# Joined quarters in the entry, transposed modulation columns, routing without GpSimd, and a split last bank

## The chip, the cores and the metric

The program runs on one core of a Trainium2 chip. The metric is the device time of one execution in microseconds (us). The engines are TensorE (PE in the profile), VectorE (DVE), ScalarE (ACT), GpSimd (POOL) and SyncE (SP), whose queue issues the loads.

## The reference

Two blocks run one after the other on 256 tokens of width 1024, all in float32. The first has two layers; each modulates a normalised input, mixes tokens (a gating, a Fourier, a differential attention and a neighbourhood group), and then lets 16 experts each take their best 32 tokens. Layer 0 does so for a context stream too.

```python
for l in range(DEPTH):                       # first block, DEPTH = 2
    mod = (s_c @ ada_w[l] + ada_b[l])[:, None, :]
    sh1, sc1, g1, sh2, sc2, g2 = jnp.split(mod, 6, axis=-1)      # and the same for the context
    hx = rms_norm(x, norm1_g[l]) * (1.0 + sc1) + sh1
    y_lat, y_ctx = token_mixers(hx, hc, w_in[l], w_out[l], ...)
    x = x + g1 * y_lat
    x = x + g2 * expert_choice_ffn(rms_norm(x, norm2_g[l]) * (1.0 + sc2) + sh2, ...)

def expert_choice_ffn(x, router_w, wg, wu, wd):
    aff = jax.nn.softmax(x @ router_w, axis=-1)
    gate, idx = lax.top_k(aff.transpose(0, 2, 1), cap)           # cap = 32
    xg = x[bidx, idx]
    hid = jax.nn.silu(xg @ wg) * (xg @ wu)
    return jnp.zeros_like(x).at[bidx, idx].add(hid @ wd * gate)

for i in range(DEPTH):                       # second block
    h = h + 0.5 * swiglu(rms_norm_2(h, ffn1_norm[i]), ...)       # width 2816
    h = h + mixer(rms_norm_2(h, mix_norm[i]))                    # a recurrence, then pooling
    h = h + 0.5 * swiglu(rms_norm_2(h, ffn2_norm[i]), ...)
    h = h + jax.nn.sigmoid(rms_norm_2(h, ple_norm[i]) @ ple_w_gate[i]) * (p[i] @ ple_w_proj[i])
return rms_norm_2(h, final_norm)
```

## The kernel before

Tokens lie on the 128 partitions in two halves (t = 0, 1), width on the free axis; for products the activations are turned by TensorE transposes into k = 8 blocks of 128 channels. Most products are made with split operands: a weight `raw` is cast to `hi` by ScalarE (L344) and the rest `lo = raw - hi` is a difference on VectorE (L345), both in pieces of 128x512; an activation is split in the same way (`hTh`, `hTl`, `T.hi`, `T.lo`), and three products are summed in PSUM. Each weight piece is a load of 1 MB, issued by SP in an order that is the order in which pieces get a slot.

The kernel's text does not stand in the order of the engines. A recording layer collects all operations, and a planner places them on each engine by phases with budgets (`phase`), by priorities, and by `issue_after`, which ties an operation's place to another. Between pieces of the mixers the generator `fill` runs products of the modulation for later parts (`ada`, L509), one load of weights at a time; `tick` says where.

Modulation. For each half of a part (512 columns), products of the conditioning vectors with `ada_w` put four partial sums of two streams into a PSUM bank of 128 partitions (partition 32c + stream). ScalarE copies it (`modp`), and four products with a constant matrix `sel` of two columns (`adc`, L490, L539) sum the four parts and turn rows into columns; VectorE adds the bias from PSUM into `mc`. There are 16 such groups: four in `ada_quarter`, ten in the mixers of layer 0 and two in those of layer 1.

Entry (`first_products`). For each quarter q of the width: `ada_quarter(q)`, transposes and modulation of both streams (`hf`, `hTh`, `hTl`), then the input products `wi` for two chunks of columns.

Route (around L1061 to L1220). After the mixers each stream has router logits, a softmax, a transposition (`afT`), four rounds of "eight largest, replace" (L1152, L1153), a comparison (L1155), a scan (L1156) and a product (L1158); `sid` turns the ranks, and `G` is a one-hot matrix with which TensorE gathers rows (`xg` to `XG`). The normalised rows are split as `xnh` (ScalarE) and `xnl` (ScalarE's `xn`, then a difference on GpSimd, L1138). `Gw`, on GpSimd too, carries the gates and is turned (`gT`, L1220) for the scatter at the end of each expert.

Second block. `T.turn(k)` (L232 to L238) turns two blocks of the normalised input and splits them; `halves_of` casts a weight chunk. The first feed-forward's start asks for the halves of the gate and the up weights, then turns T. In the last sigmoid gate, `products(n)` makes both token halves in one bank `pg`.

Of the kernel before, what the change touches and what calls it, by code (L numbers as in the profile page):

```python
# [241 lines left out]
class Prog:  # L242
# [228 lines left out]
    def ada(self, l, part, tag="ada"):  # L471
# [7 lines left out]
        def add(gi, half, b):  # L479
            m = self.t2("modp", tag="ada" if tag == "ada" else "t2")  # L480
            nc.scalar.copy(m, b)
            b = self.ps("adc", tag)
# [36 lines left out]

    def ada_quarter(self, q):  # L520
# [16 lines left out]
        b = self.ps("adc", "ada")  # L537
        for j in range(4):
            nc.tensor.matmul(b[:, 2 * j:2 * j + 2], m[:, j * 128:j * 128 + 128], self.con("sel"), start=True, stop=True)  # L539
# [9 lines left out]
    def first_products(self):  # L549
# [3 lines left out]
        self.phase(14)  # L553
        xn = {1: self.norm_rows(self.xc), 0: self.norm_rows(self.x)}
        hT, banks = {}, []
        mm = nc.tensor.matmul
        for q in range(4):
            self.ada_quarter(q)
            if q == 0:
                self.begin("w_in", 0, 0)  # L560
                self.begin("w_in", 0, 1)
                for s in (1, 0):
                    hT[s] = self.big("hTh", F32R), self.big("hTl", F32R)
            for s in (1, 0):
# [12 lines left out]
                nc.vector.tensor_tensor(l2, f, h2.bitcast(F32), ALU.subtract)  # L577
            if q == 0:
                ws = [self.halves_of("w_in", 0, c) for c in range(2)]
                banks = [{1: self.ps("wi"), 0: self.ps("wi")}, {1: self.ps("wi"), 0: self.ps("wi", "sc")}]  # L580
            for c in range(2):
                wh, wl = [v8(a) for a in ws[c]]
                for s in (1, 0):
                    hi, lo = [v8(a) for a in hT[s]]
                    for t in range(2):
                        o = banks[c][s][:, t * 256:t * 256 + 256]
                        tt = slice(t * 128, t * 128 + 128)
                        for k in (2 * q, 2 * q + 1):
                            mm(o, hi[:, k, tt], wh[:, k, :], start=k == 0 and t == 0, stop=False, skip_group_check=True)
                            mm(o, lo[:, k, tt], wh[:, k, :], start=False, stop=False, skip_group_check=True)  # L590
                            mm(o, hi[:, k, tt], wl[:, k, :], start=False, stop=k == 7, skip_group_check=True)
                if q == 3:
                    self.free(*ws[c])
            if q == 3:
                self.free(*xn.values())
        return hT, banks
# [32 lines left out]
    def mixers(self, l):  # L629
# [22 lines left out]
        def modulate(s, tags=("ps",) * 4):  # L652
# [3 lines left out]
            def evac(k0, b):  # L656
# [7 lines left out]
                ins = (nc.vector if k0 % 4 else nc.gpsimd).tensor_tensor(l2, f, h2.bitcast(F32), ALU.subtract)  # L664
# [152 lines left out]
        def diff_norm(b, j, rope):  # L817
# [3 lines left out]
            if rope:  # L821
# [12 lines left out]
                nc.gpsimd.tensor_tensor(o, o, o2, ALU.add)  # L834
# [31 lines left out]
        def inputs(grp, qT, kT, vr):  # L866
# [10 lines left out]
            for s in streams:  # L877
                b = yield from paced_rows(w, s)
# [192 lines left out]
    def route(self, l, s, res):  # L1071
# [15 lines left out]


        def evac(k0, b):
            f = self.t2("hf2")  # L1090
            for kk in range(2):
                k = k0 + kk
                fk, bk = f[:, kk * 256:kk * 256 + 256], b[:, kk * 256:kk * 256 + 256]
                if kk:
                    nc.vector.tensor_scalar(fk, bk, mc[:, 3, s, k:k + 1], None, ALU.mult)
                else:
                    nc.scalar.activation(fk, bk, AF.Copy, scale=mc[:, 3, s, k:k + 1])
# [34 lines left out]
        with self.tc.issue_after(act.ins):  # L1132
            for t in range(2):
# [14 lines left out]
        nc.gpsimd.memset(one, 1.0)  # L1148
# [18 lines left out]
    def moe(self, l, routes, loop, tail):  # L1167
# [21 lines left out]

        def gather(s):  # L1190
# [22 lines left out]
            self.free(xh, xl)  # L1213
            for t in range(2):
                gw = self.t2("Gw")
                nc.gpsimd.tensor_tensor(gw.rearrange("p (e c) -> p e c", e=E), G[t].rearrange("p (e c) -> p e c", e=E).bitcast(F32),
# [19 lines left out]
        for _ in chain(ctx, gather(0)):  # L1236
            pass

# [93 lines left out]
    def tok_part(self, bank, w, T, t, ks):  # L1332
# [5 lines left out]
        for k in ks:  # L1338
            h, l = T.hi(k)[:, c], T.lo(k)[:, c]
            mm(o, h, wh[:, k, :], start=k == 0 and t == 0, stop=False, skip_group_check=True)  # L1340
# [32 lines left out]
    def ffn(self, i, n, T, nxt, begin=None):  # L1373
# [6 lines left out]
        def products(c):  # L1380
# [8 lines left out]
            ws = [self.halves_of(f"ffn{n}_{m}", i, c) for m in "gu"]  # L1389
# [292 lines left out]
    def ple(self, i, T, nxt):  # L1682
# [4 lines left out]
        def products(n):  # L1687
            if n > 1:
                w = self.halves_of("ple_g", i, n)
                b = self.ps("pg")  # L1690
                for t in range(2):
                    self.tok_part(b, w, T, t, range(8))
# [17 lines left out]
            return banks[n]  # L1710
# [164 lines left out]
```

## Time and profile before

| | us |
|---|---|
| three runs | 2511.79, 2511.35, 2511.55 (median 2511.55) |
| profiled execution | 2511.94, of which the span 2510.2 |
| TensorE busy | 2233.8 (89%) |
| VectorE busy | 1112.3 (44%) |
| ScalarE busy | 814.7 (32%) |
| GpSimd busy | 83.9 (3%) |

The chain of work that ended last lies 59% on TensorE, 33% on loads of expert weights, 5% on VectorE. In order of time: entry to 67 us, mixers of layer 0 to about 358, routes and gathers to 416, experts to 870, mixers of layer 1 to 1062, route to 1094, experts to 1541, second block to 2499, tail. A share of the span is an average over stages with different limits, so a busy share is to be read inside a stage. In the timeline a row is one instruction or a run of like ones, with its start, its length and, in brackets, how long its engine stood idle ahead of it and what ended that.

### The profile page before, as it was taken

Reading aid. Unit: us, or ns where it says so; the run is one execution under the profiler, and the core shown is the slowest. Engines: PE = TensorE matmul, PEld = TensorE weight load, DVE = VectorE, ACT = ScalarE, POOL = GpSimd, SP = SyncE. Lnnn points to the kernel's source line nnn. Section 1 sums busy time; section 2 is a strip of 40 time slices with the busy share of each in tenths; the row PEclk is TensorE's granted clock in tenths of the full one; section 3 lists DMA queues with packets and bytes.
Section 4 is the critical chain, followed back from the end, with each engine's and each line's share of the span. In section 5 each row is a group of like instructions: output and inputs, shape, how many; then the busy total and the mean of one; then the engine's idle time right before and its main releaser. Section 6 shows DMA issues by size and latency. Waiting matters only on the chain.

```text
span 2510.2 us, 37974 instructions
## 1 busy us (share of the span) xinstructions
PE 2233.8 (89%) x15658; PEld 1587.7 (63%) x15658; DVE 1112.3 (44%) x2589; ACT 814.7 (32%) x1586; POOL 83.9 (3%) x86
## 2 busy tenths in 40 slices
PE   7999998997878889986666667999999999999998
PEld 5876684332222287742222224999989999999997
DVE  4755564121111286520101013556775566556555
ACT  3444443000000056320000002444664445445443
POOL 0000001000000010010000000000310000001000
PEclk9999998999999999986667777999999999999999
DMA  8345644999999933489999999553465555554540
GB/s 345 120 168 195 242 154 192 407 419 420 420 419 420 420 136 118 177 359 419 420 419 419 419 419 418 201 186 105 170 236 186 187 197 184 187 189 168 186 159 18
DMA packets 92797, 666.71 MB, mean 266 GB/s; under 512 B 10305, under 2 KB 10817, under 8 KB 12497
## 3 DMA queue, kind: packets, MB, share of 16 engines
q1 hardware_dynamic: 92624, 664.29, 67.4%
q8 instruction: 123, 2.02, 0.3%
q14 instruction: 50, 0.40, 0.1%
HBM read 663.20 MB, written 1.05 MB: 265 GB/s over the span
## 4 chain that ended last, share of the span: by engine, by line
PE 59%; DMA 33%; DVE 5%; ACT 2%; issue 1%; POOL 0%; SPq 0%; DVEq 0%; ACTq 0%; POOLq 0%
DMA raw<-in_e_down_dram 12%; DMA raw<-in_e_up_dram 10%; DMA raw<-in_e_gate_dram 10%; PE fg L1329 7%; PE fg L1330 7%; PE fg L1328 7%; PE acc L360 4%; PE acc L361 4%; PE acc L362 4%; PE wi L360 2%; PE wi L361 2%; PE wi L362 2%; PE yo L937 2%; PE ada L509 2%; PE eg L1252 1%; PE sc L904 1%
## 5 line engine op out<-in xcount | busy, mean ns | idle before, releaser
L345 DVE TENSOR_TENSOR lo<-raw,hi 128x512 fp32r<-128x512 f32 x748 | 484.1, 689 | 297.2 <-ACT hi L344 111.9
L344 ACT CAST hi<-raw 128x512 fp32r<-128x512 f32 x748 | 412.5, 617 | 332.6 <-DVE lo L345 107.2
L1329 PE MATMUL fg<-T,hi 128*128 128x256 f32 x1408 | 399.6, 284 | 5.9 <-DVE T L238 5.8
L1330 PE MATMUL fg<-T,lo 128*128 128x256 f32 x1408 | 399.1, 284 | 0.0
L1328 PE MATMUL fg<-T,hi 128*128 128x256 f32 x1408 | 398.9, 284 | 0.0
L1329 PEld LDWEIGHTS fg<-T,hi 128*128 128x128 f32 x1408 | 271.0, 192 | 7.8 <-DVE T L238 6.3
L1252 PE MATMUL eu<-raw,XG 128*32 128x256 f32 (+1 forms) x1536 | 212.1, 537 | 67.7 <-DMA raw<-in_e_up_dram 67.7
L1328 PEld LDWEIGHTS fg<-T,hi 128*128 128x128 f32 x1408 | 270.4, 192 | 1.5
L1330 PEld LDWEIGHTS fg<-T,lo 128*128 128x128 f32 x1408 | 271.0, 192 | 0.0
L1252 PE MATMUL eg<-raw,XG 128*32 128x256 f32 (+1 forms) x1536 | 210.6, 533 | 58.3 <-DMA raw<-in_e_gate_dram 58.3
L1252 PE MATMUL ed<-raw,hTs 128*32 128x256 f32 (+1 forms) x1536 | 215.1, 548 | 44.7 <-DMA raw<-in_e_down_dram 44.1
L1263 DVE TENSOR_TENSOR hid<-sg,eu 128x512 f32<-128x512 f32 (+1 forms) x32 | 17.7, 554 | 504.9 <-issue 332.8
L1252 PEld LDWEIGHTS eu<-raw,XG 128*32 128x32 f32 (+1 forms) x1536 | 69.1, 135 | 207.1 <-DMA raw<-in_e_up_dram 107.8
L1252 PEld LDWEIGHTS eg<-raw,XG 128*32 128x32 f32 (+1 forms) x1536 | 69.4, 134 | 197.5 <-DMA raw<-in_e_gate_dram 93.8
L1284 DVE TENSOR_TENSOR osb<-ed,g 32x512 f32<-32x512 f32 (+1 forms) x128 | 70.9, 554 | 277.3 <-PE ed L1252 267.9
L1260 ACT ACTIVATE sg<-eg 128x512 f32<-128x512 f32 (+1 forms) x32 | 15.7, 490 | 506.7 <-PE eg L1252 506.7
L1252 PEld LDWEIGHTS ed<-raw,hTs 128*32 128x32 f32 (+1 forms) x1536 | 67.5, 137 | 176.8 <-DMA raw<-in_e_down_dram 97.4
L360 PE MATMUL acc<-hi,fhh 128*128 128x512 f32 x352 | 137.7, 391 | 0.0
L361 PE MATMUL acc<-hi,fhl 128*128 128x512 f32 x352 | 137.5, 391 | 0.0
L362 PE MATMUL acc<-lo,fhh 128*128 128x512 f32 x352 | 137.0, 389 | 0.0
L360 PE MATMUL wi<-hi,hTh 128*128 128x256 f32 x384 | 116.0, 303 | 2.3 <-DVE lam L689 2.3
L361 PE MATMUL wi<-hi,hTl 128*128 128x256 f32 x384 | 112.8, 294 | 1.1 <-POOL hTl L664 1.1
(343 smaller groups left out, 3408.5 us busy)
## 6 DMA issues: line engine op xcount, KB each, us to landing
raw<-in_e_gate_dram SPq DMA_DIRECT2D x128, 1024.0 KB, 19.9
raw<-in_e_up_dram SPq DMA_DIRECT2D x128, 1024.0 KB, 19.9
raw<-in_e_down_dram SPq DMA_DIRECT2D x128, 1024.0 KB, 19.9
raw<-in_ada_dram SPq DMA_DIRECT2D x48, 1024.0 KB, 6.9
raw<-in_ffn_g_dram SPq DMA_DIRECT2D x44, 1024.0 KB, 4.9
raw<-in_ffn_u_dram SPq DMA_DIRECT2D x44, 1024.0 KB, 4.8
raw<-in_ffn_d_dram SPq DMA_DIRECT2D x44, 1024.0 KB, 4.8
raw<-in_w_in_dram SPq DMA_DIRECT2D x18, 1024.0 KB, 17.9
```

What stands on the lines that cost most here:

```text
L344: self.nc.scalar.copy(hi[:, c], src[:, c])
L345: self.nc.vector.tensor_tensor(lo[:, c], src[:, c], hi[:, c].bitcast(F32), ALU.subtract)
L360: mm(out, ah, bh, start=first, stop=False)
L361: mm(out, al, bh, start=False, stop=False)
L362: mm(out, ah, bl, start=False, stop=last)
L509: nc.tensor.matmul(b[32 * c:32 * c + 32, q * 256:q * 256 + 256], self.cs[:, k, :], v8(w)[:, k, :], start=k < 4, stop=k >= 4, tile_position ...
L937: nc.tensor.matmul(o, wT[:, k * 128:k * 128 + 128], v, start=k == 0, stop=k == nk // 128 - 1)
L1252: nc.tensor.matmul(p[M * c:M * c + M, 0:N], lhs(k), v2(w)[:, kk, c * N:c * N + N], start=k == 0, stop=k == 7, tile_position=(0, M * c))
L1284: nc.vector.tensor_tensor(ob[r:r + 32, s, c * N:c * N + N], p[q0:q0 + 32, 0:N], g2[r:r + 32, s, c * N:c * N + N], ALU.mult)
L1328: mm(o, wh[:, k, c], h, start=k == 0 and j == 0, stop=False, skip_group_check=True)
L1329: mm(o, wh[:, k, c], l, start=False, stop=False, skip_group_check=True)
L1330: mm(o, wl[:, k, c], h, start=False, stop=k == 7, skip_group_check=True)
```

## The change

Seven things are done at once.

1. Modulation columns: `ada_cols` turns `modp` with four transposes into a whole bank, and a VectorE reduction sums the four parts into an SBUF tile; the additions to `mc` read that.
2. Entry: the loop is turned by one. `ada_quarter(q)` comes first, then the products of quarter q-1 for the first chunk, then the modulation of quarter q, then the products of q-1 for the second chunk. The phase of the program's start is 12 and not 13, and 14 is not set.
3. Fills: `tick()` for `tick(2)` in the gating, and `fill(2)` ahead of each stream's input rows of group 0 in layer 0.
4. Off GpSimd in the mixers: `hTl` (L664) and the sum in L834 on VectorE.
5. Off GpSimd in the routes: `xnl` is one VectorE operation of 128x1024 (product with the scale, less `xnh`) placed behind named operations, `xnh` beside it on ScalarE without `xn`; the memset and `Gw` on VectorE. `Gw` and `gT` of both streams come after the gathers (`scatter`).
6. First feed-forward: if T isn't yet turned, only the gate weights are split first, then T's first half, then the up weights behind T's operations.
7. Tail: the last chunk of the last gate has a bank for each token half.

```diff
+    def ada_cols(self, m, tag):
+        b = self.ps("adc", tag)
+        for j in range(4):
+            self.nc.tensor.transpose(b[:, j * 128:j * 128 + 128], m[:, j * 128:j * 128 + 128], self.con("ident"))
+        r = self.small(8, "ac")
+        self.nc.vector.reduce_sum(r.rearrange("p (j s) -> p j s", j=4),
+                                  b.rearrange("p (j c r) -> p j r c", j=4, c=4)[:, :, 0:2, :], axis=AX.X)
+        return r
...
-            for j in range(4):
-                nc.tensor.matmul(b[:, 2 * j:2 * j + 2], m[:, j * 128:j * 128 + 128], self.con("sel"), start=True, stop=True)
+            b = self.ada_cols(m, tag)
...
+        for q in range(5):
+            if q < 4:
+                self.ada_quarter(q)
             if q == 0:
...
+                modulate(0)
+                self.begin("w_in", 0, 1)
...
+                continue
+            products(q - 1, 0)
+            if q < 4:
+                modulate(q)
+            else:
+                self.free(*xn.values())
+            products(q - 1, 1)
...
-                ins = (nc.vector if k0 % 4 else nc.gpsimd).tensor_tensor(l2, f, h2.bitcast(F32), ALU.subtract)
+                ins = nc.vector.tensor_tensor(l2, f, h2.bitcast(F32), ALU.subtract)
...
-                tick(2)
+                tick()
...
+                if grp == 0 and not last:
+                    self.fill(2)
...
+        def rows(t, act, dve):
+            with self.behind(act):
+                nc.scalar.activation(v2(xh)[:, t, :], v2(xt)[:, t, :], AF.Copy, scale=col[:, t:t + 1])
+            with self.behind(dve):
+                nc.vector.scalar_tensor_tensor(v2(xl)[:, t, :], v2(xt)[:, t, :], col[:, t:t + 1],
+                                               v2(xh)[:, t, :].bitcast(F32), ALU.mult, ALU.subtract)
...
+        rows(0, turned["act"], turned["dve"])
...
-        with self.tc.issue_after(act.ins):
-            for t in range(2):
-                nc.scalar.activation(v2(xh)[:, t, :], v2(xt)[:, t, :], AF.Copy, scale=col[:, t:t + 1])
-                for o in range(0, 1024, 512):
-                    n = self.t2("xn")
-                    nc.scalar.activation(n, v2(xt)[:, t, o:o + 512], AF.Copy, scale=col[:, t:t + 1])
-                    nc.gpsimd.tensor_tensor(v2(xl)[:, t, o:o + 512], n, v2(xh)[:, t, o:o + 512].bitcast(F32), ALU.subtract)
+        rows(1, act, self.short)
...
+        def scatter(s):
+            G = one_hot[s]
             for t in range(2):
                 gw = self.t2("Gw")
-                nc.gpsimd.tensor_tensor(gw.rearrange("p (e c) -> p e c", e=E), G[t].rearrange("p (e c) -> p e c", e=E).bitcast(F32),
+                nc.vector.tensor_tensor(gw.rearrange("p (e c) -> p e c", e=E), G[t].rearrange("p (e c) -> p e c", e=E).bitcast(F32),
...
-            ws = [self.halves_of(f"ffn{n}_{m}", i, c) for m in "gu"]
+            if T.done:
+                ws = [self.halves_of(f"ffn{n}_{m}", i, c) for m in "gu"]
+            else:
+                self.ahead = 0
+                ws = [self.halves_of(f"ffn{n}_g", i, c)]
+                T.turn(0)
+                T.turn(2)
+                self.norm, self.ahead = T.dve, 1
+                ws.append(self.halves_of(f"ffn{n}_u", i, c))
...
-                b = self.ps("pg")
+                b = [self.ps("pg") for _ in range(2)] if n == 3 and nxt is None else [self.ps("pg")] * 2
```

TensorE's order in the entry, about the second quarter. Before, the group of the modulation columns follows the products of `ada` at once:

```order
L532 MATMUL ada<-raw,cs 32x256 x11
L539 MATMUL adc<-k_early,modp 128x2 x4
L532 MATMUL ada<-raw,cs 32x256 x8
L568 MATMUL tr<-k_early,xn 128x128
L589 MATMUL wi<-hi,hTh 128x256 x2
L568 MATMUL tr<-k_early,xn 128x128 x4
```

and after:

```order
L541 MATMUL ada<-raw,cs 32x256 x8
L588 MATMUL wi<-hi,hTh 128x256
L589 MATMUL wi<-hi,hTl 128x256
L590 MATMUL wi<-lo,hTh 128x256
L588 MATMUL wi<-hi,hTh 128x256
L589 MATMUL wi<-hi,hTl 128x256
L590 MATMUL wi<-lo,hTh 128x256
L523 MATMUL adc<-k_early,modp 128x128 x4
L588 MATMUL wi<-hi,hTh 128x256
```

Six products of the quarter before now stand between the `ada` products and their columns.

VectorE's order in the context's route, from the scale of the softmax (`aff`) on; `xg` and `x` are the third part of the mixers' last sum into x. Before:

```order
L1130 TENSOR_TENSOR aff_3919<-rex,rrc 128x2x16
L1152 MAX m_4170<-afT 16x8
L1061 TENSOR_TENSOR xg<-wo,g_3808 128x512
L1153 MATCH_REPLACE sel<-m_4170,afT 16x256
L1064 TENSOR_TENSOR x<-x,xg 128x2x256
L1152 MAX m_4173<-sel 16x8
```

and after:

```order
L1160 TENSOR_TENSOR aff_3947<-rex,rrc 128x2x16
L1114 SCALAR_TENSOR_TENSOR xnl<-xc,rc,xnh 128x1024
L1080 TENSOR_TENSOR xg<-wo,g_3836 128x512
L1172 MEMSET sel 16x256
L1083 TENSOR_TENSOR x<-x,xg 128x2x256
L1176 MAX m_4188<-afT 16x8
L1177 MATCH_REPLACE sel<-m_4188,afT 16x256
L1176 MAX m_4191<-sel 16x8
```

The difference `xnl` has come onto VectorE ahead of the third part, and the first round of the selection from ahead of `x` to behind it.

VectorE's order at the start of the first feed-forward, from the last sums of the experts (`x<-x,cb`) on. Before:

```order
L1295 TENSOR_TENSOR x<-x,cb 128x512
L345 TENSOR_TENSOR lo<-raw,hi 128x512
L1295 TENSOR_TENSOR x<-x,cb 128x512 x3
L345 TENSOR_TENSOR lo<-raw,hi 128x512 x11
L238 SCALAR_TENSOR_TENSOR T<-tr,cols,T 128x256 x8
```

and after:

```order
L1327 TENSOR_TENSOR x<-x,cb 128x512
L345 TENSOR_TENSOR lo<-raw,hi 128x512
L1327 TENSOR_TENSOR x<-x,cb 128x512 x3
L345 TENSOR_TENSOR lo<-raw,hi 128x512 x3
L238 SCALAR_TENSOR_TENSOR T<-tr,cols,T 128x256 x4
L345 TENSOR_TENSOR lo<-raw,hi 128x512 x8
L238 SCALAR_TENSOR_TENSOR T<-tr,cols,T 128x256 x4
```

Four of T's eight second halves now stand ahead of eight of the eleven differences.

## Rows read from the trace of the kernel before

**Rows 1.** The page's slices: each digit is a tenth, 40 equal slices of the span.

```profile
PEclk9999998999999999986667777999999999999999
```

**Rows 2.** Stretches of the span: engine, busy us (instructions), granted clock, DMA share, GB/s.

```profile
416.00:870.00 454.00, 391.48 (x1656) 119.73 (x1652) 67.81 (x100) 23.00 (x38) 0.00 (x0) 0.99 1.01 418
1094.00:1541.00 447.00, 306.95 (x3138) 114.53 (x3137) 42.57 (x93) 16.52 (x40) 0.00 (x0) 0.73 1.01 419
1560.00:2499.00 939.00, 935.16 (x6563) 880.38 (x6561) 581.28 (x1050) 473.01 (x891) 48.51 (x52) 1.00 0.49 174
```

**Rows 3.** Timeline of TensorE in the entry; in brackets the idle time ahead and its releaser.

```profile
24.72 1.11 PE L568 MATMUL tr<-k_early,xn 128*128 128x128 f32 x4 [0.83 <-ACT hf L573]
37.26 1.05 PE L539 MATMUL adc<-k_early,modp 128*128 128x2 f32 x8 [0.75 <-ACT modp L536]
```

**Rows 4.** TensorE: an adc group and nine transposes; all instructions of L689.

```profile
160.16 0.95 PE L490 MATMUL adc<-k_early,modp 128*128 128x2 f32 x8
352.94 1.20 PE L433 MATMUL tr<-k_early,xc 128*128 128x128 f32 x9
L689 DVE TENSOR_REDUCE lam<-lp x2: 209/212/215, 19.6 to 885.1; 128x2 f32<-128x64 f32 x2
```

**Rows 5.** Stretches around adc groups of the mixers, same columns as group 2.

```profile
162.30:165.70 3.40, 3.40 (x17) 3.40 (x18) 2.11 (x10) 1.41 (x5) 0.00 (x0) 0.51 0.50 137
196.50:203.30 6.80, 6.80 (x25) 5.29 (x25) 3.96 (x18) 1.94 (x4) 0.00 (x0) 0.50 0.01 2
1006.00:1012.00 6.00, 6.00 (x39) 3.41 (x38) 3.80 (x19) 2.05 (x5) 0.00 (x0) 1.00 1.01 426
```

**Rows 6.** Context route: timeline, a stretch as in group 2, all L414 of one form.

```profile
372.23 2.54 POOL L1138 TENSOR_TENSOR xnl<-xn,xnh 128x512 fp32r<-128x512 f32 x2
372.30 3.02 DVE L1064 TENSOR_TENSOR x<-x,xg 128x512 f32<-128x512 f32 x1
380.02 0.67 DVE L1064 TENSOR_TENSOR x<-x,xg 128x512 f32<-128x512 f32 x1
375.24:378.11 2.87, 1.42 (x12) 1.22 (x11) 2.67 (x10) 0.00 (x0) 0.00 (x0) 1.00 0.00 0
L414 DVE SCALAR_TENSOR_TENSOR xn<-x x3: 1219/1225/1226, 15.2 to 2266.2; 128x1024 f32<-128x1024 f32 x3
```

**Rows 7.** Timeline of VectorE, GpSimd and TensorE in the x route and gather of layer 0.

```profile
378.11 0.28 DVE L1155 TENSOR_SCALAR sel<-sel 16x256 f32<-16x256 f32 x1
398.27 2.51 POOL L1138 TENSOR_TENSOR xnl<-xn,xnh 128x512 fp32r<-128x512 f32 x2
398.89 4.04 DVE L1155 TENSOR_SCALAR sel<-sel 16x256 f32<-16x256 f32 x1
408.55 0.81 DVE L1209 TENSOR_SCALAR XG<-xg,mc 128x512 f32<-128x512 f32 x1 [1.75 <-PE xg L1202]
414.52 1.03 PE L1220 MATMUL gT<-k_early,Gw 128*128 128x128 f32 x8
```

**Rows 8.** Timeline in layer 1: first modulation, then the route.

```profile
886.85 0.58 PE L361 MATMUL wi<-hi,hTl 128*128 128x256 f32 x1 [1.13 <-POOL hTl L664]
1079.31 2.07 DVE L1155 TENSOR_SCALAR sel<-sel 16x256 f32<-16x256 f32 x1
```

**Rows 9.** Timeline at the start of the first feed-forward, then two stretches of it.

```profile
1546.95 6.70 DVE L345 TENSOR_TENSOR lo<-raw,hi 128x512 fp32r<-128x512 f32 x11
1553.58 2.82 DVE L238 SCALAR_TENSOR_TENSOR T<-tr,cols,T 128x256 fp32r<-128x256 f32 x7
1554.11 0.58 PE L1329 MATMUL fg<-T,hi 128*128 128x256 f32 x1 [5.79 <-DVE T L238]
1554.20:1558.20 4.00, 4.00 (x19) 4.00 (x20) 3.46 (x8) 3.68 (x8) 0.00 (x0) 0.50 1.02 424
1562.00:1566.00 4.00, 4.00 (x35) 4.00 (x35) 1.27 (x4) 2.47 (x5) 0.00 (x0) 1.00 1.04 424
```

**Rows 10.** Timeline of ScalarE in the tail.

```profile
2498.84 0.84 ACT L1721 ACTIVATE psg<-pg,rc 128x256 f32<-128x256 f32 x2 [1.92 <-PE pg L1342]
```

More of the change, by code (lines that the diff above doesn't have):

```diff
@@ L536, in ada_quarter @@
         nc.scalar.copy(m, b)
-        b = self.ps("adc", "ada")
-        for j in range(4):
-            nc.tensor.matmul(b[:, 2 * j:2 * j + 2], m[:, j * 128:j * 128 + 128], self.con("sel"), start=True, stop=True)
+        b = self.ada_cols(m, "ada")
         k2 = slice(2 * q, 2 * q + 2)
@@ L552, in first_products, with modulate @@
         nc = self.nc
-        self.phase(14)
         xn = {1: self.norm_rows(self.xc), 0: self.norm_rows(self.x)}
-        hT, banks = {}, []
+        hT, banks, ws = {}, [], []
         mm = nc.tensor.matmul
[L557 to L563, printed above, removed]
+        def modulate(q):
             for s in (1, 0):
@@ L577, in first_products, with products @@
                 nc.vector.tensor_tensor(l2, f, h2.bitcast(F32), ALU.subtract)
+        def products(q, c):
+            wh, wl = [v8(a) for a in ws[c]]
+            for s in (1, 0):
+                hi, lo = [v8(a) for a in hT[s]]
+                for t in range(2):
+                    o = banks[c][s][:, t * 256:t * 256 + 256]
+                    tt = slice(t * 128, t * 128 + 128)
+                    for k in (2 * q, 2 * q + 1):
+                        mm(o, hi[:, k, tt], wh[:, k, :], start=k == 0 and t == 0, stop=False, skip_group_check=True)
+                        mm(o, lo[:, k, tt], wh[:, k, :], start=False, stop=False, skip_group_check=True)
+                        mm(o, hi[:, k, tt], wl[:, k, :], start=False, stop=k == 7, skip_group_check=True)
+            if q == 3:
+                self.free(*ws[c])
@@ L578, in first_products @@
+        for q in range(5):
+            if q < 4:
+                self.ada_quarter(q)
             if q == 0:
[L579 to L582, printed above, removed]
+                self.begin("w_in", 0, 0)
                 for s in (1, 0):
-                    hi, lo = [v8(a) for a in hT[s]]
-                    for t in range(2):
[L586 to L593, printed above, removed]
@@ L594, in first_products @@
-            if q == 3:
+                    hT[s] = self.big("hTh", F32R), self.big("hTl", F32R)
+                modulate(0)
+                self.begin("w_in", 0, 1)
+                ws += [self.halves_of("w_in", 0, c) for c in range(2)]
+                banks += [{1: self.ps("wi"), 0: self.ps("wi")}, {1: self.ps("wi"), 0: self.ps("wi", "sc")}]
+                continue
[3 more added lines that the diff above has]
+            else:
                 self.free(*xn.values())
+            products(q - 1, 1)
@@ L1147, in route @@
         se, sc = [q[0:E, o:o + 256] for o in (0, 256)]
-        nc.gpsimd.memset(one, 1.0)
+        nc.vector.memset(one, 1.0)
         cur = b[0:E, 0:256]
@@ L1188, in gates @@
                 self.gate_rows(l, 1, s, [g2[:, s, o:o + 512] for o in (0, 512)])
+        one_hot = {}
         def gather(s):
@@ L1237, in moe @@
             pass
+        for s in reversed(range(S)):
+            scatter(s)
         self.phase(loop)
@@ L1330, in col_part, with tok_part @@
                 mm(o, wl[:, k, c], h, start=False, stop=k == 7, skip_group_check=True)
-    def tok_part(self, bank, w, T, t, ks):
+    def tok_part(self, bank, w, T, t, ks, alone=False):
         wh, wl = [v8(a) for a in w]
@@ L1339, in tok_part @@
             h, l = T.hi(k)[:, c], T.lo(k)[:, c]
-            mm(o, h, wh[:, k, :], start=k == 0 and t == 0, stop=False, skip_group_check=True)
+            mm(o, h, wh[:, k, :], start=k == 0 and (alone or t == 0), stop=False, skip_group_check=True)
             mm(o, l, wh[:, k, :], start=False, stop=False, skip_group_check=True)
```

19 lines of the change are left out of this document (10 added, 9 removed).

## The prediction, made before the changed kernel had run

> **What bounds the kernel now.** I read the stretches first, since the shares over the whole span mix three kinds of stage. The expert stages keep the DMA engines full: 416 to 870 us and 1094 to 1541 us at a DMA share of 1.01 [rows 2]. The second block, 1560 to 2499 us, is TensorE alone, busy 935 of 939 us at full clock [rows 2]. Neither length is touched by the change. What is left is about 670 us: the entry and the mixers, two routes, the step into the second block and the tail. There the timeline is the view that counts, because a saving has to be a wait or TensorE time at that place. Time saved ahead of an expert stage is passed on, since its loads are issued as the expert products free their slots; the stage slides as a whole. Last comes the granted clock: it is not full in the slices of the second expert stage, and dips in mixers too [rows 1, 5].
>
> **Modulation columns.** A group of eight records with two moving columns took 0.95 us [rows 4]; four transposes replace it. Nine transposes in a row took 1.20 us [rows 4], 0.13 each, so four are 0.53 us. That is 0.42 us less, for 16 groups: four in the entry, ten in the mixers of layer 0, two in those of layer 1. In the mixers TensorE is the limit, so 12 x 0.42 = 5.0 us. Each group adds a reduction on VectorE; the nearest row is 0.21 us [rows 4], its results are needed much later, and VectorE has room, so I price it at nothing; if the cover fails it is 12 x 0.21 = 2.5 us. Bounds 2.5 to 5.5.
>
> **Entry.** TensorE no longer stands behind the copy of a quarter's bank: products of the quarter before lie between, and the 0.75 us wait goes [rows 3]. The four groups give 1.7. Against it, VectorE now does four lo differences ahead of the first hTh and ScalarE four casts between the context's activations. The first product can therefore come later; two lo differences are my middle estimate, each 6.70 / 11 = 0.61 us [rows 9], some 1.2, and the first wait of 0.83 [rows 3] may grow by as much. I take 0.75 + 1.7 - 1.45 = 1.0 us, bounds -1.5 to 3.5. The fills that move keep their number; they come at places where TensorE is full, so nothing.
>
> **Context route.** The GpSimd difference (a pair took 2.54 us) starts at 372.23 and the add beside it takes 3.02 us against 0.67 when alone [rows 6]. I read it as VectorE held while GpSimd works: 2.35 us that go. The new differences on VectorE are one operation of 128x1024, nearest row 1.22 us [rows 6], and they stand in front of the third xg, where VectorE now idles for TensorE. But one of the four rounds of the selection, which ran before the held add, now stands behind it: three rounds fill 375.24 to 378.11 [rows 6], 0.96 each, less the gap they used to fill, so about 0.75 comes back. Net 1.6 us; bounds 0.8 to 2.35.
>
> **x route and gather.** The last comparison of the selection took 4.04 us against 0.28 in the context's route [rows 7]: 3.76 us go with GpSimd's pair of 2.51 and the Gw behind it. One difference of 1.22 stands directly ahead of the selection, and the other splits the two G operations, which costs some 0.35 at the first XG. So 3.76 - 1.57 = 2.2 us. The second group of gT transposes stays behind the last xg, and the first eight, which ran while TensorE waited for G, join it: one more 1.03 us [rows 7]. Gw itself is four differences' worth of VectorE time in waits like the 1.75 us before an XG [rows 7]: hidden; uncovered it would be 0.67 each. Net 1.2 us; bounds 0 to 2.2.
>
> **Layer 1.** TensorE waited 1.13 us for the GpSimd hTl [rows 8]. On VectorE, first in its queue behind its own cast and at 0.67 instead of GpSimd's length, this shrinks to some 0.4; with less in the second stream, 1.0 us together, bounds 0.5 to 1.5. In the route the held comparison took 2.07 us [rows 8], 1.79 over its own 0.28, and again a 1.22 difference stands in the chain: 0.6 us, bounds 0 to 1.8.
>
> **Step into the second block.** This is the largest term. VectorE had 11 lo differences, 6.70 us, ahead of the first lo half of T, and TensorE stood 5.79 us for it [rows 9]. The order now has three of them, then four of T, then eight, then the rest of T. Eight at 0.61 are 4.9 us that leave the wait, which leaves 0.9 of 5.79. The second half of T is then ready when it was before, near 1557, and TensorE asks for it after 48 products. At half clock it had 19 products in 4 us, at full clock 35 [rows 9]; so 48 take 5.5 us at full clock and more than that at half. Beginning at 1549.6, it would meet T about then or wait up to 2 us. If the clock falls as before, the earlier products run at half rate and 2.5 us are left; if it doesn't fall since the gap is gone, up to 6.0. I take 4.5.
>
> **Tail.** Two sigmoids took 0.84 us after the last product [rows 10]; with a bank for each half the first runs earlier, and of the pairs behind them a half too: 0.7 us, bounds 0.3 to 1.0.
>
> **Sum.** 5.0 + 1.0 + 1.6 + 1.2 + 1.0 + 0.6 + 4.5 + 0.7 = 15.6 us. The profiled execution took 2511.94 us, its span 2510.2; the median is 2511.55. From the profiled run 2496.3, from the median 2495.9: I say 2496. With the bounds of each term added as independent the forecast alone has 2491 to 2501.
>
> **Rival 1: the clock gives more.** In layer 0's mixers eight of the ten groups were followed within about 3 us by half clock: 162.30 to 165.70 at 0.51 behind the group at 160.16, 196.50 to 203.30 at 0.50 [rows 4, 5]. There 17 products took 3.40 us; at the full rate of 35 in 4 us [rows 9] they take 1.9, so a stretch of 3.4 us costs 1.5. Six stretches are like the first and one like the second, so they cost 6 x 1.5 + 3.0 = 12 us; the eighth lies among waits. If the groups brought them, most go: another 8 us, 2488. Against it: TensorE there has thin work of other kinds too, and the two groups of layer 1 had full clock (1006 to 1012) [rows 5], so the groups alone do not bring it down.
>
> **Rival 2: small.** The terms overlap less with the path than I think: VectorE, which gains reductions, differences and adds, becomes the one waited for in the mixers (5.0 becomes 1.5), the entry gives nothing, the half clock stays in the step into the second block (2.5), and the routes give 2. With the tail that is some 7 us: 2505; with a little less it is no change.
>
> **Rival 3: slower, by the clock.** Suppose each of the 16 groups of transposes draws 6.8 us of half clock, like the group before 196.50 [rows 5]: 16 x 3.0 = 48 us, less the 12 already paid, is 36 us more, and 2532. It is slower than before from 47 us of additional half clock on, (15.6 + 5) / 0.44. For it speaks that a dip follows a group so often; against it that the new instructions move 128 columns and not two, and that nine transposes in a row ran at 0.13 us [rows 4].
>
> The Trainium skill's page "TensorE: Matmul & The Clock Gate", section "Part 4: PE-mode transpose", says that the full clock does not engage for transposes, which don't count as busy in the same way. By that rule rival 3 would be likelier; no row here has a group of transposes in the place of an adc group.
>
> **How the numbers follow.** The forecast has 0.56, rival 1 0.27, rival 2 0.12, rival 3 0.05. That the change doesn't do what it says is in rival 2, for the order shows each move. The range runs from 2485, rival 1 with its bound of 11 us, to 2506, with most of rival 2. A measurement here tells about 0.2%, 5 us, from no change. The forecast and rival 1 are faster by more; of rival 2 half is; so faster 0.89, same 0.06, slower 0.05.
>
> **What would show it.** TensorE's wait before its first long run of fg should fall from 5.79 to about 1 us. The comparison of the selection should take 0.28 three times, and no add near it 3 us. The four transposes of a group should take near 0.5 us, and the windows behind them tell rival 1 or 3 by their granted clock. The stretches of the experts should keep their length. I am wrong if TensorE waits for the reductions in the mixers, if the first product in the entry comes over 1.5 us later, or if the expert stage does not slide with what went ahead of it.

## The result and the profile after

The changed kernel takes 2481.80 us (median of three, 2479.56 to 2481.82) against 2511.55: 29.75 us less, a ratio of 0.9878 (0.9862 to 0.9893). The prediction was 2496 with a range from 2485 to 2506. The sign was right, the size about half, and the time lies 3 us under the range.

The page of the changed kernel, first the span and the engines' busy time, then its granted clock in 40 slices:

```profile
span 2480.0 us, 37793 instructions
PE 2203.1 (89%) x15594; PEld 1569.2 (63%) x15594; DVE 1114.8 (45%) x2628; ACT 807.0 (33%) x1574; POOL 50.2 (2%) x57
PEclk9999999999999999987677778999999999999999
```

TensorE's busy time fell by 30.7 us, as much as the span, though the products are the same but for 64 records (four fewer in each of the 16 groups). The slice row is to be read against [rows 1]: the 8 in the seventh slice, from 377 us on in the kernel before (routes and first experts), is gone. In whole tenths the dips of the mixers don't show in either row. To see where the time went I cut both executions at the same instructions in the timelines:

| stage, from and to | before | after | forecast of the change | measured |
|---|---|---|---|---|
| start to last output product `wo` of layer 0 (entry, mixers) | 376.7 | 354.0 | -5.2 | -22.7 |
| to the first expert product (routes, gathers) | 38.8 | 35.7 | -2.8 | -3.1 |
| experts of layer 0 | 454.5 | 454.1 | 0 | -0.4 |
| to the last `wo` of layer 1 | 192.3 | 190.4 | -1.8 | -1.9 |
| route of layer 1 | 31.8 | 32.8 | -0.6 | +1.0 |
| experts of layer 1 | 445.8 | 446.7 | 0 | +0.9 |
| to the end of the first feed-forward's `fg` | 192.4 | 187.5 | -4.5 | -4.9 |
| to the end of the last gate's products | 766.4 | 768.1 | 0 | +1.7 |
| tail | 11.4 | 10.8 | -0.7 | -0.6 |

One line carries the miss: the entry and the mixers of layer 0 gave 17.5 us more than the sum. The stretches of the changed kernel answer to [rows 2]; the columns are those of that group. First the expert stages and the second block, which kept their lengths, then two stretches told of below:

```profile
389.60:843.70 454.10, 390.72 (x1657) 119.34 (x1656) 67.83 (x100) 23.66 (x40) 0.00 (x0) 0.99 1.01 418
1067.00:1513.70 446.70, 297.80 (x3137) 111.51 (x3136) 41.56 (x90) 16.49 (x39) 0.00 (x0) 0.75 1.01 419
1530.40:2469.30 938.90, 935.26 (x6546) 879.80 (x6546) 585.39 (x1064) 475.57 (x898) 48.52 (x52) 1.00 0.49 175
1524.00:1528.00 4.00, 3.87 (x31) 3.58 (x30) 3.85 (x8) 3.81 (x9) 0.00 (x0) 1.00 1.00 416
1802.60:1806.00 3.40, 3.40 (x10) 2.65 (x9) 1.35 (x3) 3.40 (x11) 3.01 (x4) 0.50 0.00 0
```

### The profile page after: what moved, and what is told of

Same layout as the page of the kernel before. It is cut to its first block, busy times and chain, and to the rows that moved or that the text cites. A ratio compares the mean times of both kernels' runs of the same rounds, so it can differ in the third digit from the quotient of the medians.

```text
span 2480.0 us, 37793 instructions
## 1 busy us (share of the span) xinstructions
PE 2203.1 (89%) x15594; PEld 1569.2 (63%) x15594; DVE 1114.8 (45%) x2628; ACT 807.0 (33%) x1574; POOL 50.2 (2%) x57
## 4 chain that ended last, share of the span: by engine, by line
PE 58%; DMA 33%; DVE 5%; ACT 3%; issue 1%; POOL 0%; SPq 0%; ACTq 0%; DVEq 0%; POOLq 0%
DMA raw<-in_e_down_dram 12%; DMA raw<-in_e_up_dram 10%; DMA raw<-in_e_gate_dram 10%; PE fg L1361 7%; PE fg L1362 7%; PE fg L1360 7%; PE acc L360 4%; PE acc L361 4%; PE acc L362 4%; PE wi L360 2%; PE wi L362 2%; PE wi L361 2%; PE yo L956 2%; PE ada L508 1%; PE sc L923 1%; PE eg L1284 1%
## 5 line engine op out<-in xcount | busy, mean ns | idle before, releaser
L1284 PE MATMUL ed<-raw,hTs 128*32 128x256 f32 (+1 forms) x1536 | 209.6, 530 | 56.8 <-DMA raw<-in_e_down_dram 55.3
L1300 ACT COPY hTs<-hT 128x512 f32<-128x512 f32 (+1 forms) x32 | 15.3, 479 | 304.4 <-PE hT L1298 304.4
```

The lines of the kernel that those rows point to most:

```text
L1284: nc.tensor.matmul(p[M * c:M * c + M, 0:N], lhs(k), v2(w)[:, kk, c * N:c * N + N], start=k == 0, stop=k == 7, tile_position=(0, M * c))
```

## The experiments

**The clock in the mixers.** In every trace here the granted clock has two values, 1.00 and 0.50; half clock is the lower. Its mean between 67 and 340 us was 0.94 before and 0.98 after. The same stretch in ten kernels, in the order before, changed, and then the runs told of below (columns alone, columns undone, both, twice, dense added, thin thrice, routes alone, first feed-forward alone); the columns are those of [rows 2], so the last number but two of a row is the clock and the first in brackets counts TensorE's products:

```profile
67.00:340.00 273.00, 268.46 (x1997) 205.81 (x1996) 164.06 (x605) 125.62 (x279) 2.61 (x2) 0.94 0.49 186
67.00:340.00 273.00, 267.81 (x2079) 205.39 (x2079) 171.77 (x642) 128.60 (x287) 0.00 (x0) 0.98 0.50 191
67.00:340.00 273.00, 268.20 (x2083) 206.97 (x2082) 177.64 (x655) 133.37 (x296) 2.61 (x2) 0.99 0.51 194
67.00:340.00 273.00, 267.90 (x2022) 207.03 (x2021) 163.60 (x616) 125.27 (x281) 0.00 (x0) 0.95 0.49 186
67.00:340.00 273.00, 269.78 (x2112) 209.22 (x2111) 167.20 (x631) 127.43 (x285) 0.00 (x0) 0.99 0.48 186
67.00:340.00 273.00, 268.83 (x2122) 207.94 (x2120) 169.92 (x641) 127.97 (x285) 0.00 (x0) 0.99 0.49 189
67.00:340.00 273.00, 270.07 (x2097) 211.39 (x2096) 169.94 (x621) 131.67 (x290) 2.61 (x2) 0.98 0.50 190
67.00:340.00 273.00, 270.38 (x2032) 206.26 (x2032) 146.32 (x563) 115.17 (x254) 0.00 (x0) 0.92 0.44 165
67.00:340.00 273.00, 268.43 (x2008) 207.32 (x2007) 166.02 (x614) 127.39 (x281) 2.61 (x2) 0.95 0.50 190
67.00:340.00 273.00, 268.45 (x2002) 205.10 (x2001) 164.83 (x609) 126.10 (x281) 2.61 (x2) 0.95 0.49 186
```

TensorE is busy in all of them for 267 to 271 of 273 us. The busy time is the same and the number of products another, 1997 before and 2079 after, though not quite the same products, since the changed kernel is further on. Written as time at half clock from the trace's clock records, that is 30.9 us before, 10.2 after, and 6.8, 26.8, 6.8, 3.4, 10.2, 43.2, 27.9 and 26.7 in the others. The last two change nothing in the mixers: but for two records in the first of them, TensorE's order up to the last `wo` of layer 0 is that of before. So 27 to 31 us is the spread of one order from execution to execution.

The records leave out the start. They begin at 29.2 us before, at 20.9 in the changed kernel and between 20.8 and 32.2 in the others; ahead of that no clock is on record, and products ran at the rate of half clock. Two rows of the kernel before, on either side of 29.2 us:

```profile
28.60 0.41 PE L591 MATMUL wi<-lo,hTh 128*128 128x256 f32 x1
29.93 0.28 PE L591 MATMUL wi<-lo,hTh 128*128 128x256 f32 x1
```

Below, "with the start" means that TensorE's busy time there is counted as half clock too.

I had two theories. A: the two-column products brought the half clock, and taking them away is what gave the time. B: other parts of the change moved the work around them.

*Columns alone* and *columns undone*: the part on the modulation columns alone on the kernel before, and all but that part.

```diff
...
-            for j in range(4):
-                nc.tensor.matmul(b[:, 2 * j:2 * j + 2], m[:, j * 128:j * 128 + 128], self.con("sel"), start=True, stop=True)
+            b = self.ada_cols(m, tag)
...
```

> The kernel before with the modulation columns by transposes and the VectorE reduction, nothing else. Theory A, the two-column products brought the half clock in the mixers of layer 0: 16 groups x 0.42 us and about 10 us of clock, 2495 us (2491 to 2500), and half-granted stretches between 140 and 340 us fall from 44 us to under 15. Theory B, the dips went because other parts of the change moved the work around them: only the shorter groups count, 2506 us (2503 to 2508), and the half-granted stretches stay above 30 us.

> The changed kernel with the two-column products put back, all else as changed. Theory A: 2481.8 plus some 7 and some 10, 2498 us (2494 to 2502), with half-granted stretches behind the groups again. Theory B: 2488 us (2486 to 2490), full clock in the mixers of layer 0 nearly throughout.

Alone it took 2494.07 us, a ratio of 0.9931 (0.991 to 0.9952), 17.5 us less; undone the changed kernel took 2500.25, 0.9959 (0.9947 to 0.9971), 11.3 us under before and 18.5 over the change. The two shares, 17.5 and 11.3, add up to 28.8 of 29.75. Theory A holds against B, and the columns are worth nearly three times the 6.7 us of my sum. (The 44 us that I gave for half clock between 140 and 340 us before are 30.9 by the clock records; with the columns alone they were 6.8.) In the trace with the columns alone the stretch up to the last `wo` of layer 0 is 20.2 us shorter, 356.4 us, and that adds up: 34 us less at half clock are 15.0, at the 0.44 us each of the prediction's rivals, and 14 groups shorter by 0.35 are 4.9.

With the columns undone four of the ten groups in the mixers of layer 0 were followed by half clock, not eight. That by itself shows nothing of what stands around a group, for with TensorE's order as before the routes' run had eight and the first feed-forward's five. Here are a group and the stretch behind it in the run with the columns undone, then in the changed kernel, with the reduction:

```profile
157.40 0.95 PE L490 MATMUL adc<-k_early,modp 128*128 128x2 f32 x8
159.60:163.00 3.40, 3.40 (x17) 3.40 (x18) 2.05 (x9) 1.35 (x5) 0.00 (x0) 0.50 0.47 142
```

```profile
160.32 0.60 PE L523 MATMUL adc<-k_early,modp 128*128 128x128 f32 x4
162.60:166.00 3.40, 3.40 (x40) 1.67 (x38) 2.27 (x14) 1.99 (x6) 0.00 (x0) 1.00 0.34 72
L525 DVE TENSOR_REDUCE ac<-adc x16: 170/192/192, 22.0 to 989.9; 128x8 f32<-128x32 f32 x16
```

The group itself is 0.35 us shorter, and the stretch behind it runs at the other level of the clock. The work around it isn't the same: products of `wi` run ahead of the group in the changed kernel and behind it in the other. So the pair shows the two levels and not the cause.

*Ordinary products*: the transposes written as float32 products with the identity, so that no transpose is left in the groups, with 128 moving columns and eight records. (A product's moving columns are those of the operand that streams through; a record is one instruction in the trace.)

```diff
...
-            self.nc.tensor.transpose(b[:, j * 128:j * 128 + 128], m[:, j * 128:j * 128 + 128], self.con("ident"))
+            self.nc.tensor.matmul(b[:, j * 128:j * 128 + 128], m[:, j * 128:j * 128 + 128], self.con("ident"), start=True, stop=True)
...
```

> The changed kernel with the four transposes of each group written as ordinary float32 products with the identity: the same 128 moving columns, no transpose mode, twice the records. If few moving columns were what came before the half clock, the clock stays full in the mixers and only the longer groups cost, 16 x 0.45 us = 7 us at most: 2485 to 2490 us. If it was the length of the group, or if being transposes helps, the half clock comes back: 2494 to 2502 us.

It took 2476.78 us (0.9867, 0.985 to 0.9884), with no half clock at all between 67 and 340 us, and 8 us under what I had expected for that. A group took longer than the two-column one:

```profile
163.26 1.06 PE L523 MATMUL adc<-k_early,modp 128*128 128x128 f32 x8
```

So the length of a group isn't what came before the half clock, and being transposes isn't what kept it away. Against the transposes 14 groups longer by 0.46 us cost 6.4, yet up to the last `wo` of layer 0 the two kernels are alike, 353.8 and 354.0 us. The changed one has 17.0 us at half clock there and this one none, 7.5 us; with the start it is some 3, and the rest is open.

*Both* and *twice*: the changed kernel with additional products ahead of the transposes, written into the same bank and overwritten; two-column ones in the first, ordinary ones of 128 columns in the second.

```diff
...
         for j in range(4):
+            self.nc.tensor.matmul(b[:, 2 * j:2 * j + 2], m[:, j * 128:j * 128 + 128], self.con("sel"), start=True, stop=True)
+        for j in range(4):
             self.nc.tensor.transpose(b[:, j * 128:j * 128 + 128], m[:, j * 128:j * 128 + 128], self.con("ident"))
...
```

> The changed kernel with, ahead of each group's four transposes, the old two-column products as well, written into the same bank and overwritten. If few moving columns bring the half clock, it comes back although the transposes stand there too: 14 groups on the path x 0.89 us = 12.5 us, and some 10 us of clock, 2504 us (2500 to 2508), half-granted stretches between 67 and 340 us above 25 us. If the clock depends on what else changed, only the 12.5 us: 2494 us (2491 to 2497).

> The same with four ordinary products of 128 moving columns in place of the two-column ones: about the same added TensorE time, 14 x 1.0 us. Few columns as the cause: clock stays full, 2495 us (2492 to 2499), half-granted stretches between 67 and 340 us under 12 us. Length of the group as the cause: 2504 us and over 25 us at half.

Twice took 2491.38 us (0.9919, 0.9905 to 0.9934) with 3.4 us at half: the full clock that I expected with few columns as the cause, 0.6 us under its range. Both took 2494.67 us (0.9941, 0.992 to 0.9961), and that was a miss for theory A as I had put it: the two-column products stood there, all of them, and the half clock stayed at 6.8 us. Two-column products are not enough to bring it; with the transposes beside them it stayed away. So the theory had to be mended: the dip goes not with the two-column products by themselves but with what TensorE does at that place on the whole. Then transposes added to the groups of before should take it away, and more thin work beside the transposes of the changed kernel should bring it back. Two runs test that.

*Dense added*: the kernel before, with four transposes ahead of each group that nobody reads. *Thin thrice*: the run called both with twelve two-column products instead of four.

```diff
...
+            for j in range(4):
+                nc.tensor.transpose(b[:, j * 128:j * 128 + 128], m[:, j * 128:j * 128 + 128], self.con("ident"))
             for j in range(4):
                 nc.tensor.matmul(b[:, 2 * j:2 * j + 2], m[:, j * 128:j * 128 + 128], self.con("sel"), start=True, stop=True)
...
```

> The kernel before with four transposes ahead of each group of two-column products, into the same bank and overwritten; the two-column products still make the columns. If the clock falls because a stretch of the mixers has too little full-width work, the transposes hold it up: 14 groups x 0.53 = 7.4 us more work, 10 us less at half clock, 2508 us (2504 to 2511), half-granted stretches between 67 and 340 us under 15 us. If the two-column products or the way their result goes bring the half clock, it stays: 2519 us (2516 to 2522) and over 25 us at half.

> The changed kernel with twelve two-column products (24 records) ahead of each group's transposes, overwritten by them. Their time alone, 14 groups x 2.7 us = 37 us: 2519 us (2515 to 2523) with full clock as in the run with eight records. If little full-width work over a stretch is what counts, 2.7 us of thin work beside 0.5 us of transposes brings the half clock back: 2530 us (2525 to 2538) and over 25 us at half between 67 and 360 us.

With useless transposes added the kernel before got no slower: 2507.31 us, 0.9986 (0.9976 to 0.9995), although some 14 x 0.44 = 6.2 us of work came in (a group of the mixers took 1.39 us and not 0.95), and the half clock fell from 30.9 to 10.2 us. (In three of the ten groups of layer 0's mixers the planner put the transposes some 9 us or 5 us ahead of the products, in the others right ahead.) Thin thrice took 2572.02 us (1.0233, 1.021 to 1.0257), more than either theory said. Up to the last `wo` of layer 0 it is 60.5 us over the changed kernel: 37 are the products' time, and the half clock, 71.4 us there against 17.0, explains 54 x 0.44 = 24. The mixers of layer 1 are 26 us longer (216.7 against 190.4): two groups explain 5, and the clock most of the rest, for 44.4 us stand at half there against 10.2, some 15 us; 6 are left. Its long stretches begin behind the first group and inside the second:

```profile
1045.40:1055.60 10.20, 10.20 (x49) 4.88 (x48) 3.91 (x15) 5.30 (x11) 0.00 (x0) 0.50 0.04 14
1059.10:1086.40 27.30, 27.30 (x91) 20.12 (x91) 6.78 (x30) 8.01 (x18) 0.00 (x0) 0.50 0.00 1
```

These two runs agree with the mended theory, and so do the traces taken together. Between 67 and 340 us, 23.9 to 30.9 us stood at half in the five kernels whose groups are two-column products alone (before, columns undone, and the entry, the routes and the first feed-forward alone), and 0 to 10.2 in the six whose groups hold at least as many transposes or ordinary products of 128 columns (changed, columns alone, ordinary, both, twice, dense added). Thin thrice had 43.2. What stays open: each of these edits also made the planner move records near the groups, on TensorE at some 15 to 80 places up to the last `wo` of layer 0, so the share of the new neighbours is not separated from that of the products. It is least in both and thin thrice, with 15 and 24 places against the changed kernel. Between the run with the columns undone and the changed kernel lie 16.0 us up to the last `wo`; 13.6 us less at half clock are 6.0 of them and 14 shorter groups 4.9, and 5 are left over; with the start it is 22.8 us less, 10.0, and 1 is left.

*Again, side by side*: the changed kernel and the ordinary products on one chip.

> The changed kernel as it is, on the same chip as the next run: 2480 to 2483 us.

> Ordinary products of 128 moving columns for the transposes, again. If its 5 us under the changed kernel are real (no half clock between 67 and 340 us against 10 us of it): 2476 to 2479 us. If they were the spread of the clock from execution to execution: within 2 us of the run before.

2478.40 us (0.9873, 0.9857 to 0.989) and 2479.82 (0.9876, 0.9859 to 0.9893): the same. The 5 us between them in the first comparison were the spread from execution to execution. The traces came out as before, 10.2 us at half and none between 67 and 340 us; the longer groups take what that gives. No version here is clearly better than the change.

**The entry.**

```diff
+        for q in range(5):
+            if q < 4:
+                self.ada_quarter(q)
...
+            products(q - 1, 0)
+            if q < 4:
+                modulate(q)
...
+            products(q - 1, 1)
```

> The kernel before with the entry's loop turned and the phases of the start changed, columns as before. My sum had the entry at -0.7 us without the columns' part: 2512 us (2510 to 2514). Rival, from the run with the columns undone, where 6.7 us were won up to the last output product of the mixers: the entry takes most of it, 2506 to 2508 us.

2509.00 us, 0.9987 (0.9975 to 0.9999): 2.5 us less, where my sum had 0.7 more, and not quite the rival's 3.5. In its traced execution the stretch to the last `wo` was 7.1 us shorter, but 10.2 us less at half clock account for 4.5 of that. With the start, TensorE was busy at half for 18.0 us less, some 7.9, which leaves nothing of the 7.1 to the turned loop itself. In the changed kernel the first product came at 26.71 us, 1.2 later than before, and the wait ahead of the context's second transposes grew from the 0.83 of [rows 3] to 3.55:

```profile
23.82 2.50 DVE L345 TENSOR_TENSOR lo<-raw,hi 128x512 fp32r<-128x512 f32 x4 [1.14 <-ACT hi L344]
25.86 1.11 PE L569 MATMUL tr<-k_early,xn 128*128 128x128 f32 x4 [3.55 <-ACT hf L574]
26.24 0.42 DVE L577 CAST hTh<-hf 128x512 fp32r<-128x512 f32 x1
26.71 0.58 PE L588 MATMUL wi<-hi,hTh 128*128 128x256 f32 x1
```

The four differences ahead of `hTh` are the price I had put at 1.2, and the first product lost as much. But they came with the columns and not with the loop. Here are the differences and the first product with the columns alone, then the first product with the entry alone:

```profile
24.31 2.50 DVE L345 TENSOR_TENSOR lo<-raw,hi 128x512 fp32r<-128x512 f32 x4 [1.14 <-ACT hi L344]
27.20 0.58 PE L596 MATMUL wi<-hi,hTh 128*128 128x256 f32 x1
```

```profile
24.62 0.56 PE L581 MATMUL wi<-hi,hTh 128*128 128x256 f32 x1
```

With the entry alone the differences begin at 25.08, behind the first `hTh`, and the first product comes 0.9 us earlier than the 25.48 of before; with the columns undone it comes at 25.57.

**The routes.** The edit is the part on the routes (`rows`, `scatter`, no GpSimd) on the kernel before.

```diff
...
-                nc.gpsimd.tensor_tensor(gw.rearrange("p (e c) -> p e c", e=E), G[t].rearrange("p (e c) -> p e c", e=E).bitcast(F32),
+                nc.vector.tensor_tensor(gw.rearrange("p (e c) -> p e c", e=E), G[t].rearrange("p (e c) -> p e c", e=E).bitcast(F32),
...
```

> The kernel before with GpSimd out of the routes and the scatter's transposes after the gathers. By my sum 1.6 + 1.2 + 0.6 = 3.4 us: 2508 us. Rival, from the changed kernel, where the route of layer 1 took 1.0 us more and not 0.6 less: 2509 to 2510 us.

2510.37 us, 0.9989 (0.9978 to 0.9999): 1.2 us, beyond the rival's end, and the interval takes in what I expected. The holds went as the steps said, in the changed kernel too, where these rows of VectorE and TensorE answer to [rows 6, 7]:

```profile
353.31 0.28 DVE L1179 TENSOR_SCALAR sel<-sel 16x256 f32<-16x256 f32 x1
357.74 0.62 PE L1130 MATMUL lg<-hf,rw 128*32 128x256 f32 x2 [1.98 <-ACT hf L1126]
370.13 1.28 DVE L1114 SCALAR_TENSOR_TENSOR xnl<-x,rc,xnh 128x1024 fp32r<-128x1024 f32 x1
375.17 0.28 DVE L1179 TENSOR_SCALAR sel<-sel 16x256 f32<-16x256 f32 x1
376.75 0.26 PE L1186 MATMUL sid<-k_early,sel 16*128 16x16 f32 x2 [2.19 <-DVE sel L1182]
378.79 0.47 PE L1227 MATMUL xg<-G,xnh 128*128 128x512 f32 x1 [1.78 <-DVE G L1222]
```

The comparison takes 0.28 both times, not 4.04. So it does in every trace with GpSimd out of the routes, and in every one with it there it takes 4.03 or 4.04 in the x route. Two waits are longer or new: 1.98 us for the first `hf`, where 1.10 stood before, and 1.78 for `G`, which the transposes `gT` used to fill. The first of them before:

```profile
382.35 1.06 PE L1101 MATMUL lg<-hf,rw 128*32 128x256 f32 x2 [1.10 <-ACT hf L1097]
```

**The first feed-forward's start.**

```diff
...
-            ws = [self.halves_of(f"ffn{n}_{m}", i, c) for m in "gu"]
...
+                self.ahead = 0
+                ws = [self.halves_of(f"ffn{n}_g", i, c)]
+                T.turn(0)
+                T.turn(2)
+                self.norm, self.ahead = T.dve, 1
+                ws.append(self.halves_of(f"ffn{n}_u", i, c))
...
```

> The kernel before with the first feed-forward's start reordered (gate weights, half of T, up weights, rest of T), nothing else. Theory: the wait of 5.79 us falls to about 1 us and the clock does not fall behind it, 2505.5 to 2507 us. Rival, the half clock behind the wait stays: 2508.5 to 2509.5 us.

2507.96 us, 0.999 (0.998 to 1.0): 3.6 us, between the two. In the changed kernel the rows that answer to [rows 9]:

```profile
1521.33 1.89 DVE L345 TENSOR_TENSOR lo<-raw,hi 128x512 fp32r<-128x512 f32 x3
1523.66 0.39 PE L1361 MATMUL fg<-T,hi 128*128 128x256 f32 x1 [0.85 <-DVE T L238]
1524.94 4.89 DVE L345 TENSOR_TENSOR lo<-raw,hi 128x512 fp32r<-128x512 f32 x8
1529.76 0.87 DVE L238 SCALAR_TENSOR_TENSOR T<-tr,cols,T 128x256 fp32r<-128x256 f32 x2
```

The wait is 0.85 us and the clock behind it is full, 31 products in 4 us (1524 to 1528, above) and not 19. That won 4.9 us, in the run of this part alone 5.5. But 1.5 to 2.0 us of it are given back 280 us later, in every run with this part and in none without it. There the recurrence makes TensorE wait 3.51 us, before and after alike. First the kernel before and the stretch behind that wait, then the changed one (its stretch, 1802.6 to 1806, stands above):

```profile
1833.29 0.50 PE L360 MATMUL pp<-hi,pTh 128*128 128x512 f32 x1 [3.51 <-DVE lf L1499]
1833.50:1836.90 3.40, 3.40 (x16) 2.79 (x16) 1.12 (x2) 3.40 (x11) 3.11 (x4) 1.00 0.01 2
```

```profile
1802.16 0.50 PE L360 MATMUL pp<-hi,pTh 128*128 128x512 f32 x1 [3.51 <-DVE lf L1540]
```

Behind the same wait 16 products ran in 3.4 us at full clock before, and 10 at half clock now.

## Why the prediction was wrong, point by point

- **Modulation columns: the step that failed.** The sum gave them 5.0 us in the mixers and 1.7 in the entry, all from the groups' own length. The runs give 17.5 alone and 18.5 undone. The length was about right: 0.60 us for four transposes, not 0.53, so 0.35 and not 0.42 a group. The reduction took 0.19 us; for it or the additions behind it TensorE's products waited once, 0.7 us. What the sum left out is the clock of the products around the groups, which it took as unchanged: up to the last `wo` of layer 0, 40.8 us stood at half clock before and 17.0 after; at 0.44 us each, 23.8 us are 10.5. With the start, TensorE was busy at half for 53.6 us before and 20.9 after, and 32.7 us are 14.4, an estimate. With 14 x 0.35 = 4.9 for the groups, 19.3 of the 22.7 us are told. More than 3 are not, and the moved fills and the mixers' GpSimd work were not tried alone. They are not in waits: TensorE stood idle for 10.7 us up to the last `wo` before and for 10.3 after. I had the clock as rival 1, with its reason and rows, and gave it 0.27. The argument against it, two groups of layer 1 with full clock [rows 5], only showed that the groups do not suffice, and one execution was little for it: with the routes alone, the entry alone and the columns undone the first of these two was followed by 3.4 to 6.8 us at half. The runs show that groups alone do not suffice, and that exchanging them, with what the planner then moved, was enough in layer 0.
- **Rival 1's own price** was low too: it left out the stretch behind the eighth group, 10.2 us at half, for lying among waits, and took 8 of 12. With all 12 and 4.5 for the 10.2 us the rival's time is 2480, and a range that reached to it would have held the result.
- **Rival 3** was wrong in sign: no trace with transposes in the groups had more than 10.2 us at half between 67 and 340 us unless thin work was added. The Trainium skill's page "TensorE: Matmul & The Clock Gate", section "Part 4: PE-mode transpose", says transposes don't count as busy in the same way; here transposes that nobody reads took the half clock from 30.9 to 10.2 us, so in this place the measurement speaks against it.
- **Entry:** forecast 1.0 with its groups, so -0.7 without; alone it won 2.5 (0.3 to 6.3). The late first product was sized right but put down to the wrong edit: it came with the columns. Of the 7.1 us in its trace the clock, with the start, explains all, so what the filled waits gave is not shown.
- **Context and x route:** 2.8 forecast, 3.1 in the profile, 1.2 alone (0.3 to 5.5). The held operations went as forecast, with two waits that the sum had in part. The size is not settled by the 3.1, for with the columns alone, whose routes are as before, the same stretch was 3.8 us shorter.
- **Layer 1:** 1.8 forecast to the last `wo`, 1.9 measured. The route came out at +1.0 in one execution and -0.4 in another of the same kernel, and at +1.5 where its code was as before (columns alone). My -0.6 is neither shown nor refuted.
- **First feed-forward:** 4.5 forecast, 4.9 to 5.5 won in place and 3.2 to 3.9 kept. The mechanism was right; the half clock went where the bound of 6.0 had it, and came back at a wait I hadn't looked at.
- **Tail:** 0.7 forecast, 0.6 measured. The second sigmoid alone stands behind the last product:

```profile
2469.29 0.47 ACT L1763 ACTIVATE psg<-pg,rc 128x256 f32<-128x256 f32 x1
```

- **Expert stages:** kept their length within 0.9 us, so what was won ahead of them was passed on, as said.

## What to carry to other kernels

Price an edit to TensorE's work twice: once by its own duration, and once by the granted clock of the stretches that follow it, each with its length and its rate from the rows. Where a dip follows the same few instructions eight times in ten, that is a case of its own with full weight. Count the dips in more than one execution, for the same order gave eight here and five. The test is cheap: add work that nobody reads at that place and see whether the kernel gets slower. And after a wait is removed, look for the next wait on the same engine, for the clock can fall there instead.

## What the runs showed of the hardware

Three things I had not expected. Added TensorE work can be free: four idle transposes in each of 16 groups cost nothing on the whole, at 2507.31 us against 2511.25, since less time stood at half clock with them (10.2 us and not 30.9 between 67 and 340). Thin work can cost far more than its time: twelve instead of four two-column products a group brought 2572.02 us against 2494.67, 77 us for 16 x 1.8 = 29 us of products; in the traces 96 us more stood at half up to the last `wo` of layer 1, some 42 us. And the same wait of 3.51 us was followed by 3.4 us at half in all eight traces with the new start of the first feed-forward, which reach it between 1796 and 1882 us, and by full clock in the six without, which reach it between 1810 and 1836. So neither the wait nor the time at which it is reached decides on the dip by itself.
